# Twelve of sixteen gate chunks as Strassen units at the end of attention, with gates and mixer outputs kept in DRAM and weight sums on GpSimd

## The chip, the cores and the metric

The kernel runs on one core of a Trainium2 chip. The metric is the device time of one execution in microseconds (us). The engines are TensorE (PE in the profile, with its weight loads as PEld), VectorE (DVE), ScalarE (ACT), GpSimd (POOL) and SyncE (SP), whose queue issues nearly all DMA transfers.

## The reference

One layer of a streaming encoder, with 1024 frames of width 1024, in float32:

```
h = rmsnorm(x)
z = h @ w_in            # -> HGRN2 inputs, attention q/k/v, gate_a (1024), gate_b (1024)
oa = hgrn2_mixer(...)   # 4 heads x 128
ob = band_attention(...)  # 8 heads x 64; a chunk of 64 frames sees itself and 8 before it
merged = sigmoid(gate_a) * (oa @ w_branch_a) + sigmoid(gate_b) * (ob @ w_branch_b)
x = x + merged @ w_out
x = x + (silu(h2 @ w_gate) * (h2 @ w_up)) @ w_down          # h2 = rmsnorm(x)
x = x + sigmoid(rmsnorm(x) @ w_ple_gate) * (p @ w_ple_proj)
```

## The kernel before

Activations lie with features on the 128 partitions: `x` is 8 tiles of 128 x 1024 (8 feature blocks, 1024 frames). Every matrix product is made from float32r parts: an operand is split into a high part (a cast, on ScalarE) and a low part (the operand less its high part, on VectorE or GpSimd), and a product is three matmuls, high x high, high x low and low x high, added up in PSUM. PSUM has eight banks of 128 x 512. The usual matmul is 128 x 128 weights by 512 frames.

The stages follow one another: the first norm and the HGRN2 inputs and mixer, head by head; `attn_in`, which makes q and k; `attention`; the gates and branches; the output product; SwiGLU; its down product; the last gated embedding.

`attention` is a loop of 32 steps of two heads and 128 frames, and two more to drain. Each step runs scores, softmax, transposes and the product with v, with many short instructions on VectorE and ScalarE. Between them it takes two pieces from a `feed`, six matmuls each: the rest of `attn_in`, then two gate chunks. A block of `attn_in` (two steps) has a sum of squares on VectorE, scaled (128x8), raised to -1/2 and multiplied on GpSimd (L546, L547), and then used by VectorE to scale q and k. A step also has one wide scaling of probabilities (128x640 at the full band) on VectorE.

A gate chunk (`gate`) is 128 of the 2048 gate columns: per half of 512 frames 8 x 3 matmuls over `self.u`, the split of g*x. VectorE multiplies the PSUM result by the norm's factor `rb`. `branches` takes the other 14 gate chunks as it goes, applies the sigmoid, multiplies by the products of `oa` and `ob` with the branch weights (12 matmuls a half), and adds the two branches. Meanwhile `quad_sums` makes, on VectorE, the sums S1 to S4 of the weight blocks that the output and down products need, as Strassen (Winograd) products: 4 quads of `w_out` and 11 of `w_ffn_down`. A quad is 1 MB read, four 128x512 additions or subtractions, and 1 MB stored to DRAM.

SwiGLU already runs Strassen units (`strassen`): a unit makes two output chunks for both halves from seven products of 12 matmuls in three PSUM banks. Its operands are 2 x 2 blocks of the activations, with four of the seven being sums (T1 to T4), and sums of the weight blocks, made for the next unit by `strassen_weights` (five VectorE instructions for sums and one low part, four casts and three more low parts on other engines).

The order of the work: instructions issued through `self.V`, `self.A`, the matmul helper and `self.load` keep the order in which the code emits them on their engine (L52 is the line of the helper that pins them). Others, such as `nc.gpsimd` calls, are placed by the scheduler of the framework. Every engine, and SP's queue of transfers, works in order. Buffers come from pools: 32 `slot` tiles of 128 x 1024, four pairs of weight parts, two raw weight buffers.

Of the kernel before, what the change touches and what calls it, by code (L numbers as in the profile page):

```python
# [17 lines left out]
P = 128  # L18
T = 1024
# [13 lines left out]
AHEAD = 3  # L33

# [5 lines left out]
def f32(ap):  # L40
    return ap.bitcast(F32)
# [13 lines left out]
class Trunk:  # L55
# [429 lines left out]
    def hgrn_out(self):  # L485
        while self.pend:
            h, i, og = self.pend.pop(0)
            ps = self.mm()
            for a in range(4):
                self.tr(ps[:, a * P:a * P + P], og[:, a * P:a * P + P], self.eye)  # L490
            self.nc.scalar.activation(self.oa[h][:, i * HALF:i * HALF + HALF], ps, AF.Copy, scale=self.cols[:, C_ON:C_ON + 1])
            yield 440

# [135 lines left out]
    def attention(self):  # L629
# [3 lines left out]
        feed = chain(self.feed, self.gate(self.gates), self.gate(self.gates))  # L633
# [36 lines left out]
        for n in range(whole + 2):  # L670
# [17 lines left out]
            stage(n, 0)  # L688
            yield 0
# [3 lines left out]
    def gate(self, keep, late=False):  # L693
        (w,) = self.weights()
        t = self.slot(late=late)
# [6 lines left out]

    def branches(self):
        nc = self.nc
        ma = []
        with self.tc.issue_after(self.last.ins):
            src = [self.split(o) for o in self.oa]
        for dd in range(4):
            ts, self.gates = self.gates, []
            while len(ts) < 2:  # L710
                yield from self.gate(ts, late=True)
            if dd == 0:
                yield from self.gate(self.gates, late=True)
            (w,) = self.weights()
            for i in range(2):
                self.A.activation(ts[i], ts[i], AF.Sigmoid)
                for half in range(2):
                    hs = slice(half * HALF, half * HALF + HALF)
                    ps = yield from self.feature(w, src, half, off=i * HALF)
                    nc.vector.tensor_tensor(ts[i][:, hs], ps, ts[i][:, hs], ALU.mult)  # L720
                    yield 2592
            ma += ts
        src = [self.split(o) for o in self.ob[:2]]
        gb = []
        self.m = {}

        def some(n):
            for _ in range(n):
                yield from self.gate(gb)

        def branch(dd):
            (w,) = self.weights()
            if dd % 2 == 0:
                for kind in ("B11", "B12", "B21", "B22"):
                    self.m[kind, dd // 2] = self.slot()
            for i in range(2):
                c = 2 * dd + i
                nc.scalar.activation(gb[c], gb[c], AF.Sigmoid)
                for half in range(2):
                    hs = slice(half * HALF, half * HALF + HALF)  # L740
                    ps = yield from self.feature(w, src, half, off=i * HALF)
                    self.V.tensor_tensor(gb[c][:, hs], ps, gb[c][:, hs], ALU.mult)
                    kind = f"B{i + 1}{half + 1}"
                    (nc.gpsimd if dd < 3 else self.V).tensor_tensor(
                        self.m[kind, dd // 2][:, dd % 2 * HALF:dd % 2 * HALF + HALF], ma[c][:, hs], gb[c][:, hs], ALU.add)
                    yield 2592

        yield from some(8)
        src += [self.split(o) for o in self.ob[2:]]
        for dd in range(4):  # L750
            yield from branch(dd)
            if dd == 1:
                self.branch_sums(0)
                self.x, self.xd = [], [None] * KC
# [4 lines left out]

            if dd == 2:  # L760
# [87 lines left out]
    def quad_sums(self, src, npairs, sums, V=None):  # L848
# [3 lines left out]
        for k in range(npairs):  # L852
# [16 lines left out]
            if V is self.V:  # L869
                yield  # L870

# [727 lines left out]
    def run(self):  # L1599
# [6 lines left out]
        for dd in range(4):  # L1606
            order += [d["fm"][8 + c] for c in ((0, 1, 2), (3,), (4, 5), (6, 7))[dd]] + [d["ba"][dd]]
        order += [d["fm"][16 + c] for c in range(8)] + [d["bb"][dd] for dd in range(4)]
# [5 lines left out]
        self.es = []  # L1614

        SB, PS = bass.MemoryType.SBUF if hasattr(bass.MemoryType, "SBUF") else bass.MemoryType.SB, bass.MemoryType.PSUM
        with ExitStack() as es:
# [3 lines left out]
            self.dp = es.enter_context(tc.tile_pool(name="spill", bufs=2 * KC + 11 * STEPS + 8, space=bass.MemoryType.DRAM))  # L1621
# [8 lines left out]
            with ExitStack() as mixer:  # L1630
# [10 lines left out]
                drain(self.attention())  # L1641
            with ExitStack() as xs:
                self.late = xs.enter_context(tc.tile_pool(name="late", bufs=6))
# [155 lines left out]
```

## Time and profile before

| | |
|---|---|
| median of 3 runs | 1604.92 us (1604.38 to 1605.68) |
| span of the profiled execution | 1602.3 us |
| TensorE busy | 1579.8 us, 99% |
| VectorE busy | 1125.3 us, 70% |
| ScalarE busy | 615.3 us, 38% |
| GpSimd busy | 701.4 us, 44% |
| HBM read and written | 147.05 and 52.69 MB, 125 GB/s over the span |

The profile lists one execution. No time of its own is given beside its span; the median of the runs lies 2.6 us above it. A row of a group gives the line, engine, operation, tiles as out<-in, shapes and count, then the busy time, the mean of one in ns, and the idle time in front of them with what ended it. A row of the timeline gives start and duration in us. Matmuls overlap in the records, so TensorE's pace is read from counts in a stretch. Attention's loop takes about 336 to 527 us, the gates and branches about 527 to 800 us, SwiGLU's units up to about 1300 us.

### The profile page before, as it was taken

What the parts mean: (1) busy time and instruction counts of PE and PEld (TensorE: products, weight loads), DVE (VectorE), ACT (ScalarE), POOL (GpSimd) and SP (SyncE); (2) the same over time, 40 slices, a digit from 0 to 9 for tenths busy, and PEclk for the clock granted to TensorE, in tenths of its full rate; (3) what the DMA queues carried; (4) which work ended last, traced back from release to release, by engine and by line L of the source; (5) the groups of instructions that cost most, each with busy time, mean ns of one, the idle gap of its engine ahead of it and who ended that gap; (6) DMA issues with size and microseconds to landing.
All of it is one profiled execution on the core that took longest, in us unless ns stands there. A gap on an engine that the chain in (4) does not pass through costs nothing.

```text
span 1602.3 us, 21589 instructions
## 1 busy us (share of the span) xinstructions
PE 1579.8 (99%) x8296; PEld 1323.3 (83%) x8296; DVE 1125.3 (70%) x1731; ACT 615.3 (38%) x1031; POOL 701.4 (44%) x377
## 2 busy tenths in 40 slices
PE   8999999999999999999999999999999999999997
PEld 6998998878888888888888888888888888888886
DVE  5656656389888534323998988888888866764658
ACT  5321221177777311121376423222222233445553
POOL 3422221323122121224430777777777764644554
PEclk9999999999999999999999999999999999999999
DMA  5101000200102475653244433332333268875334
GB/s 190 53 28 53 28 28 27 86 1 28 60 2 86 152 249 188 238 165 145 80 144 171 148 115 99 99 99 99 99 108 103 84 245 312 323 273 200 125 131 158
DMA packets 69366, 201.14 MB, mean 126 GB/s; under 512 B 7824, under 2 KB 8592, under 8 KB 66832
## 3 DMA queue, kind: packets, MB, share of 16 engines
q1 hardware_dynamic: 69120, 199.75, 36.2%
q8 instruction: 65, 1.06, 0.3%
q14 instruction: 37, 0.30, 0.1%
q10 hardware_dynamic: 144, 0.02, 0.0%
HBM read 147.05 MB, written 52.69 MB: 125 GB/s over the span
## 4 chain that ended last, share of the span: by engine, by line
PE 89%; DVE 5%; ACT 1%; POOL 1%; issue 1%; DMA 0%; ACTq 0%; POOLq 0%; DVEq 0%
PE pm L81 86%; PE pm L84 3%; DVE s L52 2%; DVE m L52 2%; DVE q L52 0%; POOL wl L124 0%; ACT m L52 0%; DMA wr<-in_qk 0%; POOL m L546 0%; ACT wh L121 0%; DVE pm L52 0%; ACT s L52 0%; DVE wlo L52 0%; POOL m L472 0%; ACT t L52 0%
## 5 line engine op out<-in xcount | busy, mean ns | idle before, releaser
L81 PE MATMUL pm<-s,wh 128*128 128x512 f32 x2096 | 649.9, 391 | 5.5 <-ACT wh L121 5.2
L124 POOL TENSOR_TENSOR wl<-wr,wh 128x1024 fp32r<-128x1024 f32 (+2 forms) x120 | 297.7, 2485 | 535.5 <-ACT wh L121 524.3
L81 PEld LDWEIGHTS pm<-s,wh 128*128 128x128 f32 x2096 | 391.9, 188 | 87.3 <-ACT wh L121 5.2
L81 PE MATMUL pm<-s,wl 128*128 128x512 f32 x1048 | 408.6, 390 | 0.5 <-POOL wl L124 0.5
L81 PE MATMUL pm<-s,whi 128*128 128x512 f32 x1232 | 383.5, 392 | 0.4 <-DVE t L52 0.4
L52 DVE TENSOR_TENSOR s<-s,s 128x1024 fp32r<-128x1024 f32 (+2 forms) x203 | 250.8, 1263 | 90.9 <-ACT s L52 53.4
L81 PEld LDWEIGHTS pm<-s,whi 128*128 128x128 f32 x1232 | 231.5, 188 | 52.1 <-DVE t L52 0.8
L121 ACT CAST wh<-wr 128x1024 fp32r<-128x1024 f32 (+2 forms) x126 | 127.5, 1013 | 368.7 <-PE pm L81 148.2
L81 PE MATMUL pm<-s,wlo 128*128 128x512 f32 x616 | 241.8, 392 | 0.0
L81 PE MATMUL pm<-wh,s 128*128 128x256 f32 (+1 forms) x896 | 238.2, 340 | 0.0
L81 PEld LDWEIGHTS pm<-s,wl 128*128 128x128 f32 x1048 | 197.3, 188 | 42.1 <-POOL wl L124 1.2
L81 PEld LDWEIGHTS pm<-wh,s 128*128 128x128 f32 x896 | 154.5, 190 | 13.9 <-DVE s L339 0.2
L81 PE MATMUL pm<-wl,s 128*128 128x256 f32 (+1 forms) x448 | 147.5, 329 | 0.8 <-POOL wl L124 0.8
L81 PEld LDWEIGHTS pm<-s,wlo 128*128 128x128 f32 x616 | 115.8, 188 | 26.3 <-DVE wlo L52 0.4
L52 DVE TENSOR_TENSOR s<-pm,s 128x512 f32<-128x512 f32 (+1 forms) x118 | 76.3, 678 | 62.7 <-PE pm L81 62.6
L52 POOL TENSOR_TENSOR s<-s,t 128x512 f32<-128x512 f32 x44 | 76.7, 1744 | 86.7 <-ACT t L52 86.7
L52 ACT CAST s<-s 128x1024 fp32r<-128x1024 f32 x84 | 83.7, 1014 | 71.8 <-DVE s L52 31.5
L52 DVE TENSOR_TENSOR t<-pm,t 128x512 f32<-128x512 f32 x106 | 72.7, 686 | 53.3 <-PE pm L81 50.1
L52 ACT CAST whi<-q 128x512 fp32r<-128x512 f32 (+1 forms) x63 | 47.8, 759 | 151.8 <-DVE q L52 129.5
L81 PEld LDWEIGHTS pm<-wl,s 128*128 128x128 f32 x448 | 85.3, 190 | 6.3 <-POOL wl L124 1.0
L52 POOL TENSOR_TENSOR wlo<-wr,whi 128x512 fp32r<-128x512 f32 (+1 forms) x43 | 87.6, 2048 | 4.4 <-ACT whi L52 3.6
L546 POOL TENSOR_TENSOR m<-m,mhalf 128x8 f32<-128x8 f32 x16 | 26.6, 1663 | 122.8 <-DVE m L52 122.7
(140 smaller groups left out, 1884.1 us busy)
## 6 DMA issues: line engine op xcount, KB each, us to landing
d<-s SPq DMA_DIRECT2D x87, 256.0 KB, 2.7
s<-d SPq DMA_DIRECT2D x43, 512.0 KB, 5.9
d<-dq SPq DMA_DIRECT2D x76, 256.0 KB, 4.5
wr<-d SPq DMA_DIRECT2D x36, 512.0 KB, 3.8
wr<-in_fm SPq DMA_DIRECT2D x22, 512.0 KB, 3.3
dq<-in_wq SPq DMA_DIRECT2D x11, 1024.0 KB, 7.1
wr<-in_sg SPq DMA_DIRECT2D x22, 512.0 KB, 4.1
wr<-in_su SPq DMA_DIRECT2D x22, 512.0 KB, 4.2
```

What stands on the lines that cost most here:

```text
L52: return lambda *a, **k: self.trunk.order(op(*a, **k), self.key)
L81: return self.order(self.nc.tensor.matmul(*a, **k))
L84: return self.order(self.nc.tensor.transpose(*a, **k))
L121: self.nc.scalar.copy(hi[:, c], raw[:, c])
L124: rest.tensor_tensor(lo[:, c], raw[:, c], f32(hi[:, c]), ALU.subtract)
L546: nc.gpsimd.tensor_tensor(ss, ss, self.mhalf[:, 0:8], ALU.pow)
```

## The change

Four gate chunks stay plain: two in attention's feed, two after it. The other twelve become six Strassen units in `gate_units`, right after attention. Their activation sums come from `x`, which is loaded again (`mix_sums`). All gates go through the sigmoid and to DRAM, and come back in `branches`; `oa` and `ob` also go to DRAM and come back to be split. The weight quads are summed by `quad_slow` on GpSimd: twelve in attention, three beside the first units. `branches` has only branch products left.

```diff
+PLAIN = 4
+QUADS = 12
...
     def attention(self):
-        feed = chain(self.feed, self.gate(self.gates), self.gate(self.gates))
+        feed = chain(self.feed, self.gate(self.gates, ahead=3), self.gate(self.gates, ahead=2))
...
             stage(n, 0)
+            if n == 0:
+                self.keep_heads(self.oa, self.od, self.done_heads)
+            if n == whole // 2 + 3:
+                self.keep_heads(self.ob, self.obd, [0, 1])
             yield 0
...
+    def mix_sums(self):
...
+        load(0)
+        load(1)
+        for k in range(4):
+            xe, xo = xs[k]
+            A.activation(xo, xo, AF.Copy, scale=g(2 * k + 1))
+            yield
+            V.scalar_tensor_tensor(xo[:, h0], xe[:, h0], g(2 * k), xo[:, h0], ALU.mult, ALU.subtract)
+            V.tensor_tensor(xo[:, h1], xo[:, h0], xo[:, h1], ALU.add)
+            V.scalar_tensor_tensor(xe[:, h0], xe[:, h0], g(2 * k), xo[:, h1], ALU.mult, ALU.subtract)
+            V.scalar_tensor_tensor(xe[:, h1], xe[:, h1], g(2 * k), xo[:, h1], ALU.mult, ALU.subtract)
+            yield
+            hi, lo = self.slot(F32R), self.slot(F32R)
...
+            A.copy(hi, xo)
...
+            A.copy(hi1, xe[:, h0])
+            yield
+            V.tensor_tensor(lo, xo, f32(hi[:, :]), ALU.subtract)
+            V.tensor_tensor(lo1, xe[:, h0], f32(hi1), ALU.subtract)
+            if k < 2:
+                load(k + 2)
+            yield
...
+    def gate_done(self, c, half, ps):
+        hs = slice(half * HALF, half * HALF + HALF)
+        t = self.stmp()
+        self.V.tensor_tensor(t, ps, self.rb[:, hs], ALU.mult)
+        self.A.activation(t, t, AF.Sigmoid)
+        self.gate_keep()
+        self.kept.append((self.gd[c][:, hs], t))
...
+    def gate_units(self, sums):
...
+        side = self.mix_sums()
+        next(side)
+        self.strassen_load()
+        weights = self.strassen_weights()
...
+        for c in range(2, PLAIN):
+            (w,) = self.weights(1, ahead=PLAIN - 1 - c)
+            for half in range(2):
+                stream = self.feature(w, self.u, half, piece=2)
...
+                    next(side, None)
...
+                        next(weights, None)
+                self.gate_done(c, half, ps)
+                next(side, None)
+        drain(side)
+        drain(weights)
...
+        units = (2 * KC - PLAIN) // 2
+        for n in range(units):
+
+            def side():
+                more = self.strassen_weights() if n + 1 < units else self.branch_first()
...
+                for _ in more:
+                    if n + 1 < units:
+                        next(sums, None)
+                    yield
+
+            self.strassen(lambda c, half, ps: self.gate_done(PLAIN + 2 * n + c, half, ps), side())
+            yield 0
+        self.gate_keep()
...
+    def branch_first(self):
+        self.weights(0, ahead=3)
+        raws = self.branch_load(self.od)
...
+        for raw in raws:
+            self.osrc.append(self.split(raw))
...
     def branches(self):
...
-            while len(ts) < 2:
-                yield from self.gate(ts, late=True)
...
-        yield from some(8)
...
+    def quad_slow(self, jobs):
...
+        for n, (_, k, sums) in enumerate(jobs):
+            a11, a21, a22, a12 = cur
+            G.tensor_tensor(a22, a21, a22, ALU.add)
+            if prev:
+                store(*prev)
+            yield
+            G.tensor_tensor(a21, a11, a21, ALU.subtract)
+            yield
+            G.tensor_tensor(a11, a22, a11, ALU.subtract)
+            prev = cur, k, sums
+            if n + 1 < len(jobs):
+                cur = load(jobs[n + 1][0])
+            yield
+            G.tensor_tensor(a12, a12, a11, ALU.subtract)
+            yield
+        store(*prev)
...
-                drain(self.attention())
+                sums = self.quad_slow(jobs[:QUADS])
+                for n, _ in enumerate(self.attention()):
+                    for _ in range(2):
+                        if n > 1:
+                            next(sums, None)
+                drain(sums)
...
+                drain(self.gate_units(self.quad_slow(jobs[QUADS:])))
```

GpSimd, in attention's first steps, after the third power of `attn_in`. `m` are the small tiles of `attn_in`, `s` in the second piece are the loaded weight blocks. Before:

```order
L546 TENSOR_TENSOR m_3028<-m_3028,mhalf 128x8
L547 TENSOR_SCALAR m_3028<-m_3028,m_403 128x8
L546 TENSOR_TENSOR m_3163<-m_3163,mhalf 128x8
L547 TENSOR_SCALAR m_3163<-m_3163,m_403 128x8
L546 TENSOR_TENSOR m_3308<-m_3308,mhalf 128x8
L547 TENSOR_SCALAR m_3308<-m_3308,m_403 128x8
```

Now:

```order
L556 TENSOR_TENSOR m_3036<-m_3036,mhalf 128x8
L557 TENSOR_SCALAR m_3036<-m_3036,m_403 128x8
L1046 TENSOR_TENSOR s_3120<-s_3119,s_3120 128x512
L1050 TENSOR_TENSOR s_3119<-s_3119 128x512
L556 TENSOR_TENSOR m_3175<-m_3175,mhalf 128x8
L1052 TENSOR_TENSOR s_3119<-s_3120,s_3119 128x512
L557 TENSOR_SCALAR m_3175<-m_3175,m_403 128x8
L1057 TENSOR_TENSOR s_3120<-s_3120,s_3119 128x512
L1046 TENSOR_TENSOR s_3271<-s_3270,s_3271 128x512
L1050 TENSOR_TENSOR s_3270<-s_3270 128x512
L1052 TENSOR_TENSOR s_3270<-s_3271,s_3270 128x512
L1057 TENSOR_TENSOR s_3271<-s_3271,s_3270 128x512
```

The quads' instructions stand between the small pairs that VectorE waits for, here even inside a pair; further on whole quads, one or two, stand between two pairs.

VectorE behind attention, while TensorE runs the two plain chunks. Before, the end of attention and the branch stage, with quads (`dq`), a copy of transposed probabilities (`m`), gates read from PSUM (L700) and the splits of `oa` (L191):

```order
L861 TENSOR_TENSOR dq_5854<-dq_5854 128x512
L862 TENSOR_TENSOR dq_5854<-dq_5854 128x512
L52 COPY m_5749<-pm_5755 128x256
L700 TENSOR_TENSOR s_5713<-pm_5714,rb_436 128x512
L191 TENSOR_TENSOR s_5825<-s_1012,s_5824 128x1024
L859 TENSOR_TENSOR dq_5934<-dq_5934 128x512
L860 TENSOR_TENSOR dq_5934<-dq_5934 128x512
```

Now, from the fourth pair of `x` tiles on (`xo_6103` and `s_6102` are that pair; `q` and `wlo` weight sums and their low part; `t` a gate half read from PSUM):

```order
L54 SCALAR_TENSOR_TENSOR xo_6103<-s_6102,cols,xo_6103 128x512
L54 TENSOR_TENSOR xo_6103<-xo_6103 128x512
L54 SCALAR_TENSOR_TENSOR s_6102<-s_6102,cols,xo_6103 128x512 x2
L54 TENSOR_TENSOR wlo_6142<-q_6118,whi_6141 128x1024
L54 TENSOR_TENSOR t_6165<-pm_6106,rb_436 128x512
L54 TENSOR_TENSOR s_6170<-xo_6103,s_6169 128x1024
L54 TENSOR_TENSOR s_6135<-s_6102,s_6134 128x512
L54 TENSOR_TENSOR q_6199<-wr_6037,q_6118 128x512
```

The last activation sum that product 1 needs (`s_6170`) stands behind all sums of `x`, the first weights' sums and a gate read.

SP's queue at the same place, now (`d` are DRAM tiles: `ob` from `s_4412` and `s_4510`, the two gates of attention from `s_5533` and `s_5887`):

```order
L78 DMA wr_6035<-in_sz 128x1024
L78 DMA wr_6037<-in_sz 128x1024
L78 DMA d_6052<-s_4412 128x1024
L78 DMA d_6054<-s_4510 128x1024
L78 DMA d_6010<-s_5533 128x1024
L78 DMA d_6011<-s_5887 128x1024
L78 DMA s_6072<-in_x 128x1024
L78 DMA xo_6073<-in_x 128x1024
L78 DMA s_6102<-in_x 128x1024
L78 DMA xo_6103<-in_x 128x1024
```

The third and fourth pairs of `x` stand behind the stores of `ob` and of the gates, which wait for ScalarE.

188 lines of the change are left out of this document (142 added, 46 removed).

## The prediction

> **What bounds the kernel now.** I read the page's head and chain first, then busy time by stretches, then single rows of the stretch that the change fills. The page:
>
> ```profile
> span 1602.3 us, 21589 instructions
> PE 1579.8 (99%) x8296; PEld 1323.3 (83%) x8296; DVE 1125.3 (70%) x1731; ACT 615.3 (38%) x1031; POOL 701.4 (44%) x377
> ...
> PE 89%; DVE 5%; ACT 1%; POOL 1%; issue 1%; DMA 0%; ACTq 0%; POOLq 0%; DVEq 0%
> ```
>
> TensorE is the bound almost everywhere, so a matmul taken out is time gained unless something else then makes TensorE wait. The stretches (columns: PE, PEld, DVE, ACT, POOL busy with instruction counts, clock, DMA share, GB/s) are attention, gates and branches, and two pieces of the SwiGLU stage, which already runs Strassen units:
>
> ```profile
> 310.00:510.00 200.00, 197.68 (x1404) 164.16 (x1402) 170.82 (x592) 144.48 (x397) 54.41 (x43) 1.00 0.11 36
> 600.00:650.00 50.00, 50.00 (x222) 41.42 (x221) 21.07 (x30) 6.12 (x6) 11.04 (x5) 1.00 0.59 197
> 1000.00:1050.00 50.00, 50.00 (x219) 40.90 (x218) 42.30 (x43) 14.14 (x22) 32.87 (x19) 1.00 0.30 99
> 1050.00:1100.00 50.00, 50.00 (x219) 40.84 (x219) 44.54 (x39) 15.38 (x23) 39.74 (x23) 1.00 0.32 101
> ```
>
> In the gate stretch TensorE is full and every other engine mostly idle: 222 matmuls in 50 us, 225.2 ns each. In SwiGLU it is full as well, though VectorE is busy 42 to 45 of 50 us and GpSimd 33 to 40: 219 in 50 us, 228.3 ns each. In attention TensorE shows 99% too, but there VectorE has 85% in many short instructions, and GpSimd is idle three quarters of the time. That idle share is what the change spends.
>
> **The change part by part.**
>
> *Matmuls.* A plain gate chunk is 8 x 3 x 2 = 48 matmuls, so a pair is 96; a Strassen unit makes a pair from 7 products of 12, 84. Six units: 72 fewer. A plain pair takes 96 x 0.2252 = 21.6 us, a unit at the SwiGLU pace 84 x 0.2283 = 19.2 us: 2.44 us a unit, 14.6 us in all. At the plain pace it would be 72 x 0.2252 = 16.2 us. I take 14.6, since the units are the same code with VectorE as busy.
>
> *Weight sums taken out of the branch stage.* Their 60 VectorE instructions of about 0.69 us lie where TensorE is at 50.00 of 50; taking them out gives nothing by itself.
>
> *The same sums on GpSimd in attention.* Twelve of the fifteen quads, 48 instructions. The nearest rows for one instruction and for what GpSimd does in attention now (groups: count, busy, mean ns, idle before):
>
> ```profile
> L744 POOL TENSOR_TENSOR s<-s,s 128x512 f32<-128x512 f32 x3 | 3.9, 1294 | 3.0 <-DVE s L52 2.9
> ...
> L124 POOL TENSOR_TENSOR wl<-wr,wh 128x1024 fp32r<-128x1024 f32 x13 | 31.1, 2389 | 75.9 <-ACT wh L121 74.7 <-issue 1.3
> L546 POOL TENSOR_TENSOR m<-m,mhalf 128x8 f32<-128x8 f32 x16 | 26.6, 1663 | 122.8 <-DVE m L52 122.7
> ```
>
> 48 x 1.294 = 62 us, into idle time of 122.8 + 75.9 us: they fit. What they cost is what they make VectorE wait. The trace shows this where GpSimd was making low parts of weights (timeline rows: start, duration):
>
> ```profile
> 378.64 0.55 DVE L52 TENSOR_SCALAR m<-m,m 128x640 f32<-128x640 f32 x1
> 380.27 2.38 POOL L124 TENSOR_TENSOR wl<-wr,wh 128x1024 fp32r<-128x1024 f32 x1
> 381.85 0.15 DVE L52 TENSOR_SCALAR m<-m 128x1 f32<-128x1 f32 x1
> 383.61 2.41 POOL L124 TENSOR_TENSOR wl<-wr,wh 128x1024 fp32r<-128x1024 f32 x1 [0.95 <-ACT wh L121]
> 385.66 0.70 DVE L52 TENSOR_SCALAR m<-m,m 128x640 f32<-128x640 f32 x1
> 390.72 2.41 POOL L124 TENSOR_TENSOR wl<-wr,wh 128x1024 fp32r<-128x1024 f32 x1 [1.34 <-ACT wh L121]
> 391.88 1.27 DVE L52 TENSOR_SCALAR m<-m,m 128x8 f32<-128x8 f32 x1
> 405.98 0.23 DVE L52 TENSOR_SCALAR m<-m,m 128x8 f32<-128x8 f32 x1
> ```
>
> The 128x8 scaling took 1.27 us in place of 0.23 and ended when GpSimd's instruction did; the 128x640 one ended 0.34 us after GpSimd's end at 386.02. The 128x1 one ran through, as did the instructions that read PSUM. So of the 592 VectorE instructions of this stretch only the 128x640 scaling (one a step) and the 128x8 one (one in two steps) can be held up, by what is left of one GpSimd instruction, at most 1.3 us here. The scale starts below bound the sum over two steps, with and without GpSimd's load:
>
> ```profile
> 383.88 1.29 DVE L52 TENSOR_TENSOR m<-pm,m 128x512 f32<-128x512 f32 x2
> 398.55 1.29 DVE L52 TENSOR_TENSOR m<-pm,m 128x512 f32<-128x512 f32 x2
> 408.05 0.31 POOL L547 TENSOR_SCALAR m<-m,m 128x8 f32<-128x8 f32 x1
> 412.14 1.29 DVE L52 TENSOR_TENSOR m<-pm,m 128x512 f32<-128x512 f32 x2
> 413.92 0.56 DVE L52 TENSOR_SCALAR m<-m,m 128x640 f32<-128x640 f32 x1
> 442.56 0.31 POOL L547 TENSOR_SCALAR m<-m,m 128x8 f32<-128x8 f32 x1
> 444.72 1.29 DVE L52 TENSOR_TENSOR m<-pm,m 128x512 f32<-128x512 f32 x2
> 446.17 0.42 DVE L52 TENSOR_SCALAR m<-m,m 128x384 f32<-128x384 f32 x1
> ```
>
> 14.67 us with three weight parts (7.2 us of GpSimd) against 13.59 without: 1.08 us, nearly all of it the 128x8 row. A quad is 4 x 1.294 = 5.2 us. By the new order it mostly stands right behind GpSimd's small pair (the power and the 128x8 product), and the next wide scaling (of 640 columns, or fewer where the band is short) starts 3.3 to 5.6 us after that pair (446.17 after 442.87, 413.92 after 408.36), so it meets the quad's last instruction or none; the next 128x8 one comes after the quad. I take 0.4 us a quad, 5 us. The low end is 1 us (the next wait swallows it; a gain is excluded, since nothing leaves attention). The high end is 14 us, 1.2 us a quad. The pair itself now queues with quads: its result is waited for 3.78 us after its end in one row pair and 1.85 us in the other, more than one instruction of 1.3 us, so I put nothing on it while GpSimd keeps up. If it falls behind by a quad, this wait is late next (a rival below).
>
> *Attention's end.* Behind gate 1 the queues hold a new chain: two plain chunks on TensorE, and beside them the Strassen forms of the activations, made anew from `x`. Durations:
>
> ```profile
> L280 DVE SCALAR_TENSOR_TENSOR s<-s,cols,s 128x512 fp32r<-128x512 f32 x2 | 1.5, 752 | 2.6 <-ACT s L52 2.6
> ...
> L861 DVE TENSOR_TENSOR dq<-dq 128x512 f32<-128x512 f32 x15 | 10.4, 692 | 0.5
> L191 DVE TENSOR_TENSOR s<-s,s 128x1024 fp32r<-128x1024 f32 x8 | 9.7, 1220 | 2.8 <-ACT s L190 2.7
> ...
> 515.15 1.05 ACT L121 CAST wh<-wr 128x1024 fp32r<-128x1024 f32 x1
> ...
> 529.73 1.07 ACT L52 ACTIVATE s<-s 128x1024 f32<-128x1024 f32 x1
> ...
> s<-in_x SPq DMA_DIRECT2D x15, 512.0 KB, 7.5
> ```
>
> Count from gate 1's last matmul. TensorE needs 4 halves of 24 x 0.2252 = 21.6 us, then product 0 (its operands are there), 2.7 us; the last three matmuls of product 1, which need the fourth pair of sums, could start at 26.4 us. VectorE has by then, in order, 24 instructions of 512 columns (11 x 0.752, 13 x 0.692) and five of 1024 (1.22): 23.4 us. Two GpSimd weight parts fall into it, 1.3 and 2.4 us, which hold up instructions that read two SBUF tensors. Two waits on ScalarE add some 2 us: the fourth cast stands behind a sigmoid that waits for VectorE, and the third and fourth `x` pairs are issued behind the store of gate 1, about 2.5 us in, and land 7.5 us later, at 10, when VectorE is about to ask. So product 1 ends near 29.3 + 0.7 and TensorE waits 3 us. Unit 1's raw weights are issued behind the store of chunk 3's first half, so their sums are late by a little: 1 us more. Together 4 us; 0 if neither GpSimd nor ScalarE is met, 10 if the transfers land 5 us later and the lag goes through to unit 2. Behind those waits stand the PSUM reads of the plain chunks; a unit holds three of eight banks, so TensorE does not feel them.
>
> *Later units.* GpSimd has four weight parts a unit and, in units 0 to 2, a quad: 7 x 1.294 + 2.4 = 11.5 us in 19.2, 60%, under the 66 to 79% of the SwiGLU rows, where the matmul count holds. Cost 0.
>
> [...]
>
> *Hand-over to the branches.* `oa` and the gates come back from DRAM:
>
> ```profile
> s<-d SPq DMA_DIRECT2D x43, 512.0 KB, 5.9
> ```
>
> The `oa` tiles are asked for early in the last unit (19.2 us), behind three weights; splits of 1.05 + 1.22 us each follow. I take 1 us, ends 0 and 4 (the third weight waits for a raw buffer). In the branches only transfers are added: some 16 MB in 32 half chunks of 2.7 us, 186 GB/s, which the 197 GB/s row carried without a loss.
>
> *Sum.* -14.6 + 5 + 4 + 1 = -4.6 us. The profiled span of 1602.3 becomes 1597.7; the median of the three runs, 1604.92, lies 2.6 us above that span, so 1600.3 us. The likeliest case's own range is 1596 to 1605.
>
> **The rivals.**
>
> 1. *All of the work is hidden.* VectorE's waits in attention fall where it waits for TensorE anyway, and GpSimd's two parts miss it at attention's end: -14.6 + 1 + 0 + 0 gives 1591.3, at the plain pace 1589.7. For it: a quad mostly ends before the next wide scaling. Against it: at 170.82 of 200 us VectorE has little time in which to catch up.
>
> 2. *Slower: GpSimd falls behind in attention.* GpSimd works in order. If a quad's load lands late, the quad blocks the power behind it, VectorE stops at the scaling of q and k, and TensorE behind it. A delay of a whole quad less the spare time, 5.2 - 2.8 = 2.4 us, in 12 blocks is 29 us: 1602.3 + 2.6 - 14.6 + 29 + 5 = 1624. It decides from 14.6 - 5 = 9.6 us on, 0.8 us a block. For it: two quads stand ahead of one power in three places, 10.4 us in some 11 to 13 us. Against it: 36 GB/s in attention leaves the transfers free.
>
> 3. *The units starve.* VectorE and GpSimd stay late through the six units, by 2 us each: 1600.3 + 8 = 1608, no gain (the change then does not do what it says). For it: unit 0 starts with VectorE behind. A unit's VectorE instructions with two SBUF inputs (seven of 0.69, one of 1.22 us) and GpSimd's 11.5 us, one after the other, are 17.6 of 19.2 us. Against it: SwiGLU keeps 219 matmuls with more work beside them. [...]
>
> **How the numbers follow.** A difference under 0.2%, 3.2 us, can't be told from none here: faster is below 1601.7, slower above 1608.1. The forecast has 0.48, the first rival 0.2, the second 0.17, the third 0.15. Faster: 0.2 and three quarters of 0.48, 0.56. Same: most of the rest of the forecast, a third of the third rival and a little of the second, 0.2. Slower: 0.24. Leaving out one in ten at each end, the range goes from the first rival's 1590 to 1613, inside which the second rival's milder half lies.
>
> **What would show it.** Right: 72 fewer matmuls; attention longer by about 5 us, with 128x640 scalings of 0.7 to 1.7 us; one hole of TensorE of about 3 us in the first unit, on VectorE's or ScalarE's sums; 219 matmuls in 50 us after that. Wrong: scalings of q and k that wait for GpSimd (rival 2); holes at the start of each unit (rival 3); no longer attention (rival 1); or a hole where the branches wait for `oa` or a gate, which I price at 1 us.

## The result, and the profile after

The changed kernel takes 1603.58 us (median of 20 runs, 1601.64 to 1607.84), the kernel before 1605.04 us (20 runs, 1604.38 to 1607.14): a ratio of 0.9992, with a 95% interval from 0.9985 to 0.9999. That is a gain of 1.5 us, below the 0.2% that the prediction took for a difference, and 3.3 us short of the forecast of 1600.3.

The profiled execution of the changed kernel spans 1600.6 us, against 1602.3 before. Its page's head and the shares of its chain of work:

```profile
span 1600.6 us, 21819 instructions
PE 1568.0 (98%) x8224; PEld 1309.6 (82%) x8224; DVE 1173.3 (73%) x1759; ACT 643.7 (40%) x1085; POOL 796.5 (50%) x449
```

The 72 matmuls are gone (8296 to 8224), and TensorE is busy 11.8 us less. Of these the span shows 1.7. The stretches that answer to those in the prediction (attention, the Strassen units that now make the gates, and SwiGLU):

```profile
310.00:510.00 200.00, 194.74 (x1366) 160.58 (x1365) 171.59 (x580) 140.66 (x389) 117.00 (x91) 1.00 0.57 190
600.00:650.00 50.00, 50.00 (x219) 40.89 (x218) 34.08 (x37) 19.02 (x30) 28.00 (x18) 1.00 0.50 169
1000.00:1050.00 50.00, 50.00 (x219) 40.88 (x218) 42.36 (x41) 13.32 (x20) 34.89 (x20) 1.00 0.33 107
```

The units run as SwiGLU does, 219 matmuls in 50 us with TensorE full. In attention GpSimd went from 54 to 117 us of 200, and TensorE from 197.68 to 194.74. The time can be followed by three marks of the trace: the first and the last copy of an attention output from PSUM, and the first product of SwiGLU.

| stretch | before, us | after, us | difference | predicted |
|---|---|---|---|---|
| start to first copy (code not changed) | 337.00 | 337.68 | +0.68 | 0 |
| first to last copy (attention) | 190.20 | 194.04 | +3.84 | +5 |
| last copy to first SwiGLU product | 323.8 | 317.3 | -6.5 | -14.6 + 4 + 1 |
| from there to the end | 751.3 | 751.6 | +0.3 | 0 |

In the third row, TensorE's starts lie up to 5 us apart between 560 and 600 us; before, no start in that place was late. What these gaps and the slow matmuls behind the longest add over 0.23 us a matmul is 8.1 us, and -14.6 + 8.1 gives the -6.5. So the matmul term holds, and what is missing is at attention's end: 8.1 us lost, where the prediction had 4. The waits of TensorE between 530 and 850 us (what was waited for: us in total, times, longest):

```profile
PE pm L83 <- DVE t L54: 5.8, 2, 4.9
```

The page's timeline shows the long one. Rows of TensorE, VectorE and ScalarE of the changed kernel (start, duration; idle time before and what ended it):

```profile
567.41 0.39 PE L83 MATMUL pm<-s,wlo 128*128 128x512 f32 x1
572.69 1.22 PE L83 MATMUL pm<-s,whi 128*128 128x512 f32 x2 [4.89 <-DVE t L54]
```
```profile
566.48 1.28 DVE L54 TENSOR_TENSOR t<-pm,rb 128x512 f32<-128x512 f32 x2
569.41 2.62 DVE L54 TENSOR_TENSOR s<-s,s 128x512 fp32r<-128x512 f32 x4 [1.65 <-ACT s L54]
571.96 0.68 DVE L54 TENSOR_TENSOR t<-pm,t 128x512 f32<-128x512 f32 x1
```
```profile
568.24 0.62 ACT L54 ACTIVATE t<-t 128x512 f32<-128x512 f32 x1
568.77 2.16 ACT L54 CAST s<-s 128x512 fp32r<-128x512 f32 x4
570.84 0.57 ACT L54 COPY t<-pm 128x512 f32<-128x512 f32 x1
```

The matmul at 567.41 is the last of product 2 in unit 0, the one at 572.69 the first of product 3. Product 3 adds into the second of the unit's three banks (`b2`), which holds product 1. The row of VectorE at 571.96 is the one that reads it first (`u2`, product 0's copy plus product 1): TensorE must not add until it has ended, 572.64, and starts at 572.69. `u2` in turn stands on VectorE behind the four last low parts of `x` (`mix_last`), and needs ScalarE's copy of product 0, which stands behind the four casts of the same. Both stand behind the two PSUM reads of plain chunk 3 and their sigmoids.

### The profile page after: what moved, and what is told of

Read it like the earlier page. It is cut to its first block, busy times and chain, and to the rows that moved or that the text cites. A ratio compares the mean times of both kernels' runs of the same rounds, so it can differ in the third digit from the quotient of the medians.

```text
span 1600.6 us, 21819 instructions
## 1 busy us (share of the span) xinstructions
PE 1568.0 (98%) x8224; PEld 1309.6 (82%) x8224; DVE 1173.3 (73%) x1759; ACT 643.7 (40%) x1085; POOL 796.5 (50%) x449
## 4 chain that ended last, share of the span: by engine, by line
PE 81%; DVE 9%; POOL 2%; ACT 1%; issue 1%; DMA 1%; SPq 0%; POOLq 0%; DVEq 0%; ACTq 0%
PE pm L83 79%; DVE s L54 4%; DVE m L54 3%; PE pm L86 2%; DVE q L54 1%; POOL m L556 1%; ACT s L54 0%; DVE pm L54 0%; DMA d<-s 0%; DVE t L54 0%; ACT m L54 0%; DMA s<-in_oq 0%; POOL wl L126 0%; DVE wlo L54 0%; DMA wr<-in_fm 0%
## 5 line engine op out<-in xcount | busy, mean ns | idle before, releaser
L83 PE MATMUL pm<-s,wh 128*128 128x512 f32 (+1 forms) x1712 | 532.1, 392 | 5.6 <-ACT wh L123 5.4
L83 PE MATMUL pm<-s,whi 128*128 128x512 f32 x1568 | 489.6, 393 | 7.1 <-DVE t L54 7.0
L83 PEld LDWEIGHTS pm<-s,wh 128*128 128x128 f32 x1712 | 319.7, 189 | 72.9 <-ACT wh L123 5.9
L83 PEld LDWEIGHTS pm<-s,whi 128*128 128x128 f32 x1568 | 295.3, 189 | 74.0 <-DVE t L54 8.3
L83 PE MATMUL pm<-s,wl 128*128 128x512 f32 (+1 forms) x856 | 333.8, 390 | 0.5 <-POOL wl L126 0.5
L54 DVE TENSOR_TENSOR s<-s,s 128x512 f32<-128x512 f32 (+4 forms) x213 | 257.5, 1237 | 92.7 <-ACT s L54 55.2
L83 PE MATMUL pm<-s,wlo 128*128 128x512 f32 x784 | 308.3, 393 | 0.4 <-POOL wlo L54 0.4
L83 PEld LDWEIGHTS pm<-s,wl 128*128 128x128 f32 x856 | 161.2, 188 | 34.7 <-POOL wl L126 1.5
L54 ACT CAST s<-s 128x1024 fp32r<-128x1024 f32 (+1 forms) x94 | 90.2, 980 | 67.4 <-DVE s L54 33.5
L54 POOL TENSOR_TENSOR wlo<-q,whi 128x512 fp32r<-128x512 f32 x54 | 90.5, 1676 | 53.0 <-ACT whi L54 39.2
```

Of the source, the lines that this page charges most:

```text
L54: return lambda *a, **k: self.trunk.order(op(*a, **k), self.key)
L83: return self.order(self.nc.tensor.matmul(*a, **k))
```

## The experiments

Times are medians, beside runs of the kernel before on the same chip, whose medians were 1604.7 to 1604.9 us throughout. Two explanations of the long wait were set against each other. Theory A: it is the order of the instructions around the bank. Theory B: VectorE is late by the work of the sums, as the prediction had it, and would be wherever the eight instructions stand.

**1. The last low parts behind the read of the bank** (e1_low_late).

```diff
-        for hi, _, x in self.mix_last:
-            A.copy(hi, x)
-        for hi, lo, x in self.mix_last:
-            V.tensor_tensor(lo, x, f32(hi), ALU.subtract)
...
                 if n == 0:
                     yield
+                    for hi, _, x in self.mix_last:
+                        A.copy(hi, x)
+                    for hi, lo, x in self.mix_last:
+                        V.tensor_tensor(lo, x, f32(hi), ALU.subtract)
                     yield
```

> The four casts and four differences that make the last low parts of x (mix_last) stand behind the read of bank 2 in unit 0, not ahead of it; nothing else moves. Theory A (product 3 adds into bank 2 and so waits for VectorE's read of it, which stands behind these eight instructions): the wait of 4.9 us ahead of product 3 falls to about 2.4 us, since the read still waits for ScalarE's copy of product 0 behind two sigmoids (567.2 to 568.9 in the changed kernel) and 0.6 us for that copy; the stretch at half clock behind it (1.6 us) goes. TensorE's lost time between 560 and 600 us goes from 8.1 to about 4 us, the run to about 1599.5 us, 5.5 below the kernel before. Theory B (VectorE is simply late from the sums, wherever they stand): a wait of 4 us or more stays, there or one product later, and the run is within 1 us of the changed kernel's 1603.6.

Measured: 1600.26 us, ratio 0.9972 (0.9962 to 0.9982). The wait ahead of product 3, in the timeline of this run:

```profile
569.57 0.72 PE L83 MATMUL pm<-s,whi 128*128 128x512 f32 x2 [2.33 <-DVE t L54]
570.13 0.40 PE L83 MATMUL pm<-s,wlo 128*128 128x512 f32 x1
```

The wait is 2.33 us, as theory A had it, and the matmul behind it takes its usual time. A gap of 1.6 us start to start turned up from 575.0 on, ahead of product 5, which adds into the same bank again and waits for the next read of it. So 5.4 us were lost in all, not 4: VectorE carried some of its lateness on, as theory B has it.

**2. The reads of chunk 3 behind it as well** (e2_reads_late, and the same kernel again, e2_again). Beside the edit of run 1:

```diff
-                self.gate_done(c, half, ps)
+                if c + 1 < PLAIN:
+                    self.gate_done(c, half, ps)
+                else:
+                    held.append((c, half, ps))
...
                         V.tensor_tensor(lo, x, f32(hi), ALU.subtract)
+                    for h in held:
+                        self.gate_done(*h)
                     yield
```

> As the run before, and the two PSUM reads of plain chunk 3 with their sigmoids go behind the read of bank 2 as well. Theory A: the copy of product 0 now stands behind no sigmoid, the read of bank 2 comes within 0.7 us of the end of product 1, and no wait over 0.5 us is left in unit 0: lost time between 560 and 600 us about 1.5 us (the hole of 1.1 us in unit 1 stays), the run about 1597 us, 8 below the kernel before. Theory B: VectorE is late by the same work, so the wait turns up at product 4 or 5 of unit 0 or grows in unit 1 to 3 us or more, and the run stays above 1600 us.

Measured: 1597.16 us, ratio 0.9955 (0.9941 to 0.9969). TensorE's waits between 530 and 620 us:

```profile
PE pm L83 <- DVE t L54: 0.7, 1, 0.7
```

1.4 us are lost in the units in place of 8.1. Product 3 is still the place, since ScalarE's copy of product 0 stands behind a cast that waits 2.55 us for a weight sum of VectorE. The hole of 1.1 us in unit 1 went with it. No other wait took the place: theory A is right, and theory B has at most what was left in run 1.

> The same kernel as run e2_reads_late, on the same chip as the two runs beside it, so that these two can be set against it: about 1597.2 us.

Measured: 1596.30 us, ratio 0.9946 (0.9934 to 0.9959).

**3. GpSimd's sums left out** (e3_no_quad_work): the four `tensor_tensor` calls of `quad_slow` are taken out, its loads and stores stay.

```diff
-            G.tensor_tensor(a22, a21, a22, ALU.add)
             if prev:
                 store(*prev)
             yield
-            G.tensor_tensor(a21, a11, a21, ALU.subtract)
             yield
-            G.tensor_tensor(a11, a22, a11, ALU.subtract)
             prev = cur, k, sums
...
-            G.tensor_tensor(a12, a12, a11, ALU.subtract)
```

> The changed kernel without GpSimd's 60 instructions for the later weights' sums: the loads and the stores stay, in the same order, and the unsummed quarters are stored, so the output isn't the reference's. If attention's 3.84 us more (first to last copy of the attention outputs, 190.2 before and 194.0 after) are VectorE's waits for GpSimd, they go: 190.2 to 190.8 us, 128x640 scalings back at 0.61 us and 128x8 ones at 0.31. If they come from the transfers or from the slots, attention stays at 193.5 to 194.5. In unit 1 the hole of 1.1 us (VectorE's sums held up by GpSimd, which was behind by one quad) goes as well, the 5 us hole in unit 0 stays. The run: 1603.6 - 3.5 - 1.1, about 1599; 1602.5 by the transfers.

Measured: 1598.80 us, ratio 0.9965 (0.9952 to 0.9978). Attention takes 190.77 us, 0.6 more than in the kernel before. The scalings of VectorE in attention (340 to 530 us; count, busy, mean ns, idle before) in the kernel before, the changed one and this one:

```profile
L52 DVE TENSOR_SCALAR m<-m,m 128x640 f32<-128x640 f32 x16 | 9.7, 606 | 0.6
L52 DVE TENSOR_SCALAR m<-m,m 128x8 f32<-128x8 f32 x13 | 4.0, 310 | 0.5
L52 DVE TENSOR_SCALAR m<-m,m 128x512 f32<-128x512 f32 x4 | 1.9, 487 | 0.1
```
```profile
L54 DVE TENSOR_SCALAR m<-m,m 128x640 f32<-128x640 f32 x16 | 11.5, 720 | 0.6
L54 DVE TENSOR_SCALAR m<-m,m 128x8 f32<-128x8 f32 x13 | 5.2, 402 | 0.5
L54 DVE TENSOR_SCALAR m<-m,m 128x512 f32<-128x512 f32 x4 | 3.6, 903 | 0.1
```
```profile
L54 DVE TENSOR_SCALAR m<-m,m 128x640 f32<-128x640 f32 x16 | 9.2, 574 | 0.6
L54 DVE TENSOR_SCALAR m<-m,m 128x8 f32<-128x8 f32 x13 | 4.0, 308 | 0.5
L54 DVE TENSOR_SCALAR m<-m,m 128x512 f32<-128x512 f32 x4 | 2.0, 488 | 0.1
```

The loads and stores by themselves cost attention 0.6 us at most; its other 3.3 us come with GpSimd's instructions. No store waits for a sum in this run either, so what a late store holds up in SP's queue goes with them. One such place may be copy 24 (counted from 0), where the changed kernel takes 8.28 us to the next copy, the kernel before 6.98 and this run 6.92. GpSimd's last sum in attention had ended at 474.5, 11 us before. ScalarE waits 2.46 us ahead of the cast of a weight, by the profile for its load, and then VectorE for ScalarE:

```profile
488.97 1.05 ACT L123 CAST wh<-wr 128x1024 fp32r<-128x1024 f32 x1 [2.46 <-DMA wr<-in_fm]
```
```profile
491.81 0.35 DVE L54 SCALAR_TENSOR_TENSOR s<-pm,cols,s 128x128 fp32r<-128x128 f32 x1 [1.26 <-ACT m L54]
```

Why that cast comes late was not tested. The 5 us hole of unit 0 stays (5.27 us start to start), and the one of unit 1 goes.

**4. The same sums in halves** (e4_halved): each 128x512 instruction as two of 128x256.

```diff
+            def two(out, x, y, op):
+                for i in range(2):
+                    s = slice(i * D // 4, i * D // 4 + D // 4)
+                    G.tensor_tensor(out[:, s], x[:, s], y[:, s], op)
+
-            G.tensor_tensor(a22, a21, a22, ALU.add)
+            two(a22, a21, a22, ALU.add)
```

> Each of GpSimd's 128x512 instructions for the later weights' sums as two of 128x256; the same data and transfers. A 128x512 one takes 1.30 us and a 128x1024 one 2.39, so one of 256 columns should take some 0.75 us. If VectorE waits for what is left of one GpSimd instruction, its waits about halve: attention 192 to 192.8 us in place of 194.0, the run about 1602. If what counts is how long GpSimd is busy in all (1.5 in place of 1.3 us for each 512 columns), attention grows to 194.5 or more, and the run is at 1604 or above.

Measured: 1605.66 us, ratio 1.0005 (0.9996 to 1.0015). The wide scalings (128x640 and 128x512) get shorter and attention gets longer, 197.1 us. Groups of this run, and VectorE's waits for GpSimd's pair of small instructions in the changed kernel and in this one:

```profile
L54 DVE TENSOR_SCALAR m<-m,m 128x640 f32<-128x640 f32 x16 | 9.9, 620 | 0.6
L1049 POOL TENSOR_TENSOR s<-s,s 128x256 f32<-128x256 f32 x70 | 50.1, 745 | 13.8 <-DMA s<-in_wq 6.6 <-DMA d<-s 4.1 <-DMA s<-in_oq 3.1
```
```profile
DVE m L54 <- POOL m L557: 1.8, 3, 1.2
```
```profile
DVE m L54 <- POOL m L557: 4.8, 3, 1.9
```

So there are two costs. One is what is left of one GpSimd instruction when VectorE wants to scale, which halving makes smaller: VectorE's scalings together take 1.3 us less than in the changed kernel. The other is GpSimd's being late with the power and the small product that VectorE needs, which grew by 3.0 us. That it grows with GpSimd's busy time is argued, from this run alone. And 1.5 of the 3.1 us that attention lost are not of the halving itself: behind a wait of TensorE of 1.83 us, which the changed kernel has as well, the clock fell to half in this trace and not in that one, and two steps took 1.5 us longer (the last section has the rows).

**5. The sums elsewhere** (e5 to e11, all with the edits of run 2). The edits change `QUADS`, the step from which attention draws instructions, and how many are drawn at a place.

```diff
-QUADS = 12
+QUADS = 8
...
-                        if n > 1:
+                        if n > 13:
                             next(sums, None)
...
-                    if n + 1 < units:
-                        next(sums, None)
+                    for _ in range(2):
+                        if 0 < n < units - 1:
+                            next(sums, None)
```

> The kernel of run e2_reads_late, with the later weights' sums in other places: 8 of 15 groups in attention, begun at step 14 of 32 in place of step 2, and the other 7 in the four middle units, two instructions at each place in place of one. Theory A (the sums cost only where GpSimd also has weights' low parts or waits for transfers: between copies 5 and 13 of the attention outputs, and 24): the 2.5 to 3 us of the first half go, the 1.3 us at copy 24 stays, attention is 191.5 us in place of 195.3, the units keep 19.3 us, and the run is about 1593.5 us, 3.5 below e2_reads_late. Theory B (each group costs its 0.3 us wherever it stands, and in the units VectorE and GpSimd, at some 14 of 19.3 us each, fall behind): attention falls by 1 us only or the units grow to 20 us or more, and the run is at 1597 or above.

Measured: 1603.06 us, ratio 0.9989 (0.9980 to 0.9997). Neither theory: attention takes 199.5 us, 9.3 more than in the kernel before. Up to copy 22 it loses 1.3 us, at copies 23 and 24 another 2.2, and then 5.8 at one step. Rows of SP's queue, GpSimd and VectorE there:

```profile
484.10 2.69 SPq L78 DMA_DIRECT2D wr<-in_fm  x2
486.84 0.90 SPq L78 DMA_DIRECT2D s<-in_wq  x2
```
```profile
494.52 1.27 POOL L1052 TENSOR_TENSOR s<-s,s 128x512 f32<-128x512 f32 x1 [3.57 <-DMA s<-in_wq]
495.74 1.67 POOL L556 TENSOR_TENSOR m<-m,mhalf 128x8 f32<-128x8 f32 x1
497.38 1.27 POOL L1056 TENSOR_TENSOR s<-s 128x512 f32<-128x512 f32 x1
498.62 0.32 POOL L557 TENSOR_SCALAR m<-m,m 128x8 f32<-128x8 f32 x1
```
```profile
498.97 1.29 DVE L54 TENSOR_TENSOR m<-pm,m 128x512 f32<-128x512 f32 x2 [4.72 <-POOL m L557]
```

The queue issues nothing from 472.8 to 484.1, where it stands at a weight whose buffer isn't free. The load of the next group is behind it, GpSimd's sum waits for that load, the power waits behind the sum, VectorE for the power. That is the second rival of the prediction, at a single place: 4.7 us on VectorE, 5.4 on TensorE, and a stretch at half clock behind it. In the units GpSimd was busy 19.5 to 19.7 of each 20 us from 600 to 660 and ended the last sum at 662.4, when the last unit had begun. The loads of the branches stood in the queue behind its stores, and TensorE lost another 3.1 us at the hand-over.

> The kernel of run e2_reads_late with the later weights' sums in three places, where the runs before showed them to cost nothing: 5 groups in attention, begun at step 14 and ended by step 24 (no weight and no late transfer stands beside them there), 6 in units 0 to 4, 4 in the second half of the branches. If the sums cost by place (GpSimd beside weights' low parts, or a load held in the queue behind a weight's), attention falls to 190.5 to 191 us, as in the run without the sums, the units stay at 19.3 us, the hand-over to the branches has no hole over 0.5 us, and the run is about 1593 us. If each group has its price wherever it stands, it is at 1596 or above; if GpSimd is still behind at the last unit, the branches begin 1 to 3 us late, as in run e5_second_half.

Measured: 1613.67 us, ratio 1.0059 (1.0045 to 1.0073), the worst of all; 5 groups in attention, 6 in the units, 4 in the branches. Attention was as expected, 190.85 us with five groups between steps 14 and 24. But units 2 and 3 took 25.4 and 23.9 us. SP's queue and VectorE in unit 2:

```profile
591.01 3.27 SPq L79 DMA_DIRECT2D d<-s  x4
596.03 1.62 SPq L79 DMA_DIRECT2D s<-in_wq  x2
597.74 0.86 SPq L79 DMA_DIRECT2D wr<-in_sz  x2
```
```profile
606.91 1.57 DVE L55 TENSOR_TENSOR q<-wr,wr 128x512 f32<-128x512 f32 x1 [6.58 <-DMA wr<-in_sz]
```

The stores of a group wait in the queue for GpSimd, the raw weights of the next unit stand behind them, and VectorE waits 6.6 us for these: the third rival, through the transfer queue and not through VectorE's own work. In the branches another 7.7 us went, with VectorE 7.6 us behind GpSimd's sums of the branch outputs.

> The kernel of run e2_reads_late with the later weights' sums placed by what the runs before showed: 8 groups in attention (3 at steps 2 to 8, 5 at steps 14 to 24; none where a weight or a late transfer stands beside them), 4 in the units at one instruction a place, and 3 in the branches, there on VectorE as in the kernel before. If the price of the sums is one of place, attention is 191 to 192 us (190.8 without the sums, 193.7 to 195.3 with twelve), the units keep 19.3 us, the branches have no hole, and the run is about 1594 us, 2.5 below e2_again. If every group costs 0.3 us wherever it stands in attention, 1595.5. If GpSimd's stores in the units hold up the units' weights in the transfer queue (as they did in e7_spread at two instructions a place), holes of 3 to 5 us before product 3 of unit 2 or 3, and the run above 1598.

> As e8_places, with 3 groups in the units, at the pace of the changed kernel, and 4 in the branches on VectorE. By place the run is about 1594 us, as e8_places; it is the safer of the two if the fourth group in the units puts its stores ahead of a unit's weights, and the dearer one if the branches, whose transfers already take 296 of some 400 GB/s at their start, can't carry a fourth group: then TensorE has a hole behind a gate or a weight that came late, and the run is above 1595.

Measured: e8_places 1595.83 us, ratio 0.9947 (0.9933 to 0.9960); e9_vector 1603.49 us, ratio 0.9990 (0.9982 to 0.9999). From attention's end to SwiGLU e8 has no hole but unit 0's 1.4 us. In attention it loses 3.3 us, as much as twelve groups do, half of it at one step (+1.55 us at copy 13), so the price by place isn't as simple as that expectation had it. The expectation's "some 400 GB/s" is a rate that the traces show: from 695 to 700 us the changed kernel's transfers ran at 420 GB/s. In e9 the fourth group in the branches made VectorE wait for its load (735.8 to 743.3):

```profile
DVE s L1052 <- DMA s<-in_wq: 7.5, 1, 7.5
```

VectorE was behind from there on. At 766 two of its sums took 2.2 and 3.4 us beside GpSimd's low parts, and TensorE waited 3.8 us for them in the output projection.

> As e8_places, with all of attention's groups in its second half and closer together: 7 from step 14, three instructions a step in place of two, so that the last load is issued ahead of the queue's stop at a weight (484 us); 5 groups in the units, 3 in the branches on VectorE. If the second half is free (it was, with 5 groups at two a step: 190.85 us), attention is 191 to 191.5 us and the run 1593.5 us. If three instructions a step make the scale of q and k wait for GpSimd, attention is 193 us or more, as in e8_places, and the run 1596 or above.

> As e10_seven, with 8 groups in attention's second half and 4 in the units. If the second half is free up to the queue's stop, attention is 191 to 191.5 us and the run 1593.5 us, as e10_seven. If the eighth group's load falls behind the stop at the weight, a hole of 4 to 6 us near 495 us, as in e5_second_half, and the run 1598 to 1600 us.

Measured: e10_seven 1596.77 us, ratio 0.9955 (0.9943 to 0.9968), attention 193.55 us: with three instructions a step it costs what the other placings cost. e11_eight 1602.56 us, ratio 0.9985 (0.9976 to 0.9994), attention 194.8 us with 3.4 us of it at copy 23. Its profiled execution was the shortest of its eleven, 1598.16 us, so 4.4 us of the median are not in its trace, and what they are stays open.

**6. One unit less** (e6_five_units): `PLAIN = 6`, two more plain gates at attention's end.

```diff
-PLAIN = 4
+PLAIN = 6
...
-self.gate(self.gates, ahead=3), self.gate(self.gates, ahead=2))
+*[self.gate(self.gates, ahead=3) for _ in range(PLAIN - 3)], self.gate(self.gates, ahead=2))
```

> The kernel of run e2_reads_late with five units in place of six: chunks 4 and 5 stay plain, two of the plain gates more at attention's end. It prices the matmul term by itself. By the starts of units 2 to 5 of the changed kernel a unit takes 19.32 us and a plain pair of chunks 21.6, so the run should be 2.3 us longer than e2_reads_late, about 1599.5 us, with 12 matmuls more. If a unit also costs something that doesn't show in TensorE's starts (a hand-over, VectorE's lateness carried on), the difference is under 1.5 us; if the sixth unit hides waits of its own, over 3 us.

Measured: 1600.03 us, ratio 0.9965 (0.9951 to 0.9978), 3.7 us over e2_again, not 2.3. Its profiled execution, at 1601.94 us, is the longest of its five. There attention itself took 197.3 us against 193.7, with the same 1392 matmuls from first to last copy; 1.5 us of this is a stretch at half clock behind a wait of 1.83 us. From attention's last copy to the last product of the units it is 147.9 us against 144.4, of which 1.0 us is lost in unit 0 (2.5 against 1.5 us): 2.4 us are left for the unit.

Twelve groups placed as in the change cost attention 3.4 to 5.1 us (193.6 to 195.3 us in four traces: the changed kernel, e1, and e2 twice), and 7.1 us in e6. Seven or eight in other places cost 3.1 us (e9) to 9.3 us (e5); only five, between steps 14 and 24, cost next to nothing (0.65 us in e7). What makes the difference between five and seven in the same half is open. The fastest versions, e2_reads_late, e8_places and e10_seven, lie some 8 to 9 us below the kernel before and can't be told from each other.

## Why the prediction was right and wrong

*Matmuls, -14.6 us: right.* 72 are gone. By the starts of the changed kernel units 2 to 5 take 19.32 us each, where 19.2 was taken from SwiGLU's pace, and run 6 gives 2.4 us a unit.

*Attention, +5 us: the mechanism right in part, the size in part by luck.* It measured +3.84, and from 3.4 to 7.1 in the other executions with the same groups; without GpSimd's sums it is +0.6. The lengthened scalings are there (128x640 from 606 to 720 ns, 128x512 from 487 to 903). But there is no one price a quad, as the 0.4 us had it: five quads cost 0.65 us in e7, and 1.3 of the 3.84 us lie at copy 24, where no sum was running and ScalarE waited ahead of a weight's cast. And that GpSimd's pair was given nothing "while GpSimd keeps up" was on the edge: VectorE waits for it 1.8 us in place of 1.1, and in halves, with 15% more of busy time on the sums (e4), 4.8.

*Attention's end, +4 us, 1 of it in unit 1: wrong, and this is the step that failed.* It measured 8.1. The prediction said of the PSUM reads behind VectorE's waits: "a unit holds three of eight banks, so TensorE does not feel them". Free banks were counted, and there are enough. What was not seen is that a unit adds into the same bank again, two products later, so that the read of product 1 is due within one product's time, 2.8 us, whatever other banks are free. The wait looked for at product 1, on the sums of its operands, is 0.3 us (start to start 0.51 us at 563.8). The one at product 3 is 4.9 us, and the half clock behind it another 1.6. Run 1 and run 2, which change nothing but the order around that read, take 3.3 and 6.4 us off the run, and the losses between 560 and 600 us go from 8.1 to 5.4 and 1.4.

The 1.3 and 2.4 us for GpSimd's weight parts in the estimate of VectorE's lateness were met. Rows of the changed kernel: two kinds of VectorE instruction on SBUF tensors, first beside no part of GpSimd, then each beside one:

```profile
549.74 1.42 DVE L54 SCALAR_TENSOR_TENSOR s<-s,cols,xo 128x512 f32<-128x512 f32 x2
553.53 0.69 DVE L54 TENSOR_TENSOR s<-s,s 128x512 fp32r<-128x512 f32 x1
555.69 2.77 POOL L54 TENSOR_TENSOR wlo<-wr,whi 128x1024 fp32r<-128x1024 f32 x1 [6.54 <-ACT whi L54]
556.25 3.43 DVE L54 SCALAR_TENSOR_TENSOR s<-s,cols,xo 128x512 f32<-128x512 f32 x2
564.13 1.28 POOL L54 TENSOR_TENSOR wlo<-q,whi 128x512 fp32r<-128x512 f32 x1 [5.67 <-ACT whi L54]
564.19 1.77 DVE L54 TENSOR_TENSOR s<-s,s 128x512 fp32r<-128x512 f32 x1
```

They took 2.0 and 1.1 us longer, and an instruction beside a third part (547.79 to 549.15) took 1.67 in place of 0.69: 4.1 us where the estimate had 3.7.

*Unit 1, 1 us: the size right by luck, the reason incomplete.* 1.0 us at 593.3. It was put on the raw weights behind a store. It goes away without GpSimd's sums (e3), and also without the lateness of unit 0 (e2), so it took both.

*Later units, 0: right for this placing.* They keep 19.32 us each. Not right in general: at two instructions a place e7 lost 10.7 us in units 2 and 3.

*Hand-over to the branches, +1 us: 0.* No gap over 0.3 us between starts from 600 to 850 us.

*The weight sums taken out of the branch stage, 0: not separated by a run.* The stage ran full before and after. (The prediction gives each of the 60 instructions 0.69 us; two of their four groups, L859 and L862, have a mean of 0.84 in the kernel before. Nothing rests on it.)

*The rivals.* The first (all hidden, 1591) didn't come. The second and third did not decide this kernel, but each was met in part in a kernel with the sums elsewhere, by SP's order of transfers both times: a load held behind a weight (e5), a weight held behind a store (e7). That the third puts VectorE's sums and GpSimd's "one after the other" is borne out by the row at 564.19: 1.77 us in place of 0.69, with its end 0.55 us behind that of GpSimd's part, 565.41.

The sum: -4.6 us predicted and -1.7 in the profiled span. Attention gave 1.2 us and the hand-over 1.0 back, attention's end took 4.1 more, and 1.0 us lies in stretches that were not changed, where the kernel before lost some 1.4 us to a slow clock that the changed one did not (last section). So it is in part luck that the 1603.6 us still lie inside the 1596 to 1605 of the likeliest case: two terms that came out low pay for half of the one that was missed.

## What to carry to other kernels

Where a bank is added into more than once, its read between two products is a deadline for the reading engine: here TensorE waited 4.9 us for one that was late. List what stands ahead of that read on VectorE and ScalarE, and put what is due later behind it: eight casts and differences and two PSUM reads, moved by a few places in the order, were worth 6.4 us, four times what the change gained by itself. The work given to an idle engine was paid for where another engine waited for its small results (VectorE 4.8 us in e4), and where its loads and stores stood in a transfer queue ahead of something that was due (VectorE 6.6 us in e7).

## What the hardware showed

TensorE was slow for a while after each long wait, and after some short ones. Rows of the stretches of the changed kernel around the long wait (columns as above, granted clock the third number from the end), and the timeline behind it:

```profile
567.60:572.60 5.00, 0.20 (x1) 0.00 (x0) 3.35 (x6) 3.82 (x8) 1.27 (x1) 0.99 0.70 204
572.60:575.80 3.20, 3.11 (x7) 2.48 (x8) 1.15 (x3) 0.62 (x1) 1.28 (x1) 0.50 1.00 344
575.80:580.00 4.20, 4.20 (x20) 3.43 (x19) 3.06 (x6) 0.60 (x2) 0.00 (x0) 0.99 0.91 369
```
```profile
574.13 1.05 PE L83 MATMUL pm<-s,whi 128*128 128x512 f32 x2
574.99 0.63 PE L83 MATMUL pm<-s,wlo 128*128 128x512 f32 x1
...
576.33 0.63 PE L83 MATMUL pm<-s,whi 128*128 128x512 f32 x2
```

For some 3.2 us the granted clock is 0.50, and matmuls start 427 ns apart in place of 226 to 233. So this wait of 5 us cost 6.6 us. The same wait cost 7.9 us in e3, where the clock stood at 0.50 for 6 us, from 569 to 575.

The clock also fell behind start-to-start gaps of 3.30, 4.68 and 5.39 us (e7), 4.22 (e9), 5.29 (e4) and 5.67 (e5). It did not behind one of 2.72 us, 2.33 of them idle (e1). A gap of 2.10 us in attention, 1.83 of them idle, left it whole in three traces (the changed kernel, e1 and e2_reads_late) and halved it in two (e4 and e6). The rows of e4, the wait and the stretch behind it:

```profile
499.22 0.69 PE L86 MATMUL pm<-eye,m 128*128 128x128 f32 x2 [1.83 <-DVE m L54]
```
```profile
499.20:502.40 3.20, 3.18 (x9) 2.14 (x9) 2.90 (x13) 1.57 (x3) 0.96 (x1) 0.50 0.32 86
```

The kernel before has such a stretch with no idle time over 0.26 us ahead of it, behind 16 matmuls of one column in the SwiGLU stretch; the changed kernel ran the same 16, and what follows them, at a clock of 1.00:

```profile
876.23 1.84 PE L81 MATMUL pm<-ones,s 128*128 128x1 f32 x16
```
```profile
878.70:882.00 3.30, 3.30 (x9) 2.62 (x8) 3.27 (x4) 2.23 (x5) 2.23 (x1) 0.50 0.27 102
```

The slow stretches lasted from 3.2 to 6 us at a clock of 0.50. An idle time of 1.83 us stood ahead of one in two of five traces, and one of 2.33 us (e1) ahead of none. So these traces show no length of wait below which the clock is safe, and the same 16 matmuls with what follows them took some 1.4 us longer in one trace than in the other.
